# Another order of the seven block products of values and gates, and four pieces of work moved beside them

## The chip, the cores and the metric

The kernel runs on one core of a Trainium2 chip. The metric is the device time of one execution in microseconds (us), lower is better. The engines named here are TensorE (PE), the vector engine (DVE), the scalar engine (ACT), GpSimd (POOL), which here only issues DMAs, and SyncE (SP), whose queue loads the weights.

## The reference

One layer of a decoder with two branches that read the same normalised input: 512 tokens, model width 1024, all in fp32.

```python
proj = rms_norm(x, norm_mix) @ w_in
rq, rk, rv, rg, cq, ckv, krope, gr, gm = jnp.split(proj, offsets, axis=-1)
# retention: 4 heads, 256 wide in q and k, 512 in v, decay per head
ro = retention(rope(rq), rope(rk) * 256 ** -0.5, rv)
ro = rms_norm(ro, ret_norm)                 # per head
a_ret = (ro * silu(rg)) @ w_br
# latent attention: 8 heads, q from cq, k and v from ckv, rotary key krope shared
a_mla = causal_block_attention(q, k, v) @ w_bm
mixed = sigmoid(gr) * a_ret + sigmoid(gm) * a_mla
x = x + mixed @ w_o
x = x + square(relu(rms_norm(x) @ w_up)) @ w_down
x = x + sigmoid(rms_norm(x) @ w_ple_gate) * (p @ w_ple)
```

The change touches the retention part (`rv`, `rg`, the scores, the product with `w_br`) and, in two places, the preparation of the attention's keys.

## The kernel before, in words

**Matmuls in three parts.** An fp32 operand is split into a high part (ACT, L260 for weights, a rounding copy to the PE's fp32r type) and a low part (DVE, the difference: L264, or L266 where the weight is taken with the sign turned, which is the case for products 1 and 4). A product is then three matmuls, low by high, high by low, high by high, all on line L167 (`MM`). Names: `wr_` is the raw weight tile, `wh_` and `wl_` its high and low part; `xn0h`, `xn0l` are those of the normalised input.

**The order of the work.** A list of steps is written out by hand (`step(key, fn, ...)`), and `run_steps` goes through it. A step with a key uses one weight chunk of 512 KB; before the step runs, its chunk and the next one are split (`AHEAD` is 1), and, for the chunks of the products, the next three are loaded (`PREP` is 3). Matmuls stay in this written order; each other engine gets its instructions in an order that a scheduler makes from the same list, and works it off in order. There are 6 raw tiles (`NRAW`) and 3 of each part (`NW`).

**Values and gates by seven products.** For each pair of heads q = 0, 1 the values (`rv`) and then the gates (`rg`) are one matrix product of 2 x 2 blocks, computed with seven block products instead of eight (`ret_seven`). The operands made from the inputs are `xn` and sums of them (`s30`, `s50`, `s60`, `s70`...); those of the weights are made on the way to the chip. Each product p has two chunks c = 0, 1, with 12 matmuls each. The order before is 1, 7, 2, 6, 4, 5, 3. `wr_rv071` is chunk 1 of product 7 of the values of pair 0.

- Weights: SP loads 1, 2, 3 alone. 7 is loaded by SP, and POOL adds a second block to it (an accumulating DMA, L222). 6 has no tile of its own: POOL adds a block to 7's tile once 7 has been split, and 4's to the same tile once 6 has been split. 5 is loaded by SP and added to by POOL.
- PSUM: 1, 6, 5, 3 accumulate one after the other in the same two banks (chain a), 7 and 4 in two others (chain c), 2 in two of its own (b).
- Take-out (`seven_out`): after 1, 7 and 6 ACT copies the banks out (L749); after 2, 5 and 4 DVE adds them to what was taken out before (L754, tiles `cv` for values and `z` for gates, `_11`, `_21`, `_22` by block); after 3 ACT finishes the last block (L793, L785 with the silu for gates). The next product of a chain can start when the former has been taken out.

**Retention around it.** `qk(h, "rq", n)` and `"rk"` are projections of 24 matmuls with a rotary on DVE behind them (L809 to L816, then the split L306: `rqx`, `rqy`). `ret_scores` is 24 smaller matmuls (`rs`), loads the head's decay tile `dec` on SP's queue (L822), multiplies by it (L830) and splits the result (`ath`, `atl`). `ret_attend` multiplies scores and values (`ro`), `ret_gated` (L851, on DVE) multiplies the output `o` by its norm and by the gates `z`, `ret_turned` turns it with 16 transposes on PE (`ot`) and splits it with a gain (`rog`, ACT L308, DVE L311), and `branch_r` (`br`) multiplies it by `w_br`, in four steps of 24 matmuls each for a head. `gate_r` (`gr`) are eight projections for the branch's gate, `EARLY` of them in the first part of the kernel.

**The attention's part.** `scores` goes block by block over four blocks of queries (`sc`), six matmuls a block; `head_factor(h)` (`pbk`) spreads the norm factors of head h's keys with four transposes, from `hr`, which DVE works out (L602); `rotary_key` spreads a factor in the same way (`prho`) and makes the shared rotary key. `fill(n)` puts in n half projections of the gates (`gm`, later `gr`), 12 matmuls each.

Of the kernel before, what the change touches and what calls it, by code (L numbers as in the profile page):

```python
# [54 lines left out]
NDYN, NKEEP, NW, NRAW, NDRAW, AHEAD, PREP, EARLY, PAD = 45, 16, 3, 6, 4, 1, 3, 5, 104  # L55
# [91 lines left out]
def trunk_layer(ctx: ExitStack, tc: tile.TileContext, xT, pT, pos, gains, const, decay, wstream, outT):  # L147
# [58 lines left out]
    def step(key, fn, *args):  # L206
        steps.append((key, fn, args))
# [906 lines left out]
    def fill(n=1):  # L1114
        for _ in range(n):
            if fillers and fillers[0][0] is None:
                step(*fillers.pop(0))
            if fillers:
                step(*fillers.pop(0))
# [17 lines left out]
    step(("qr", 0), query_rotary, 0)  # L1137
    step(None, mask_parts)
    step(None, rotary_out, 0)
    fill(1)  # L1140
    step(None, rotary_key)
    fill(2)
    step(None, rotary_stats, 0)
    step(None, pair_sums, 0)
    fill(1)
# [6 lines left out]
    for h in range(MH):  # L1152
        p, more = h // 2, h + 2 < MH
        if h % 2 == 0 and h:
            step(None, scores, h, (0, 1))
            step(None, head_factor, h)
            step(None, scores, h, (2, 3))
            step(None, head_factor, h + 1)
        else:
            step(None, scores, h)  # L1160
        if h % 2 == 0:
            if more:
                step(("kq", h + 2), kq_head, h + 2)
            else:
                fill(2)
            if h:
                step(None, attend, h - 1)
            if more:
                step(("kq", h + 3), kq_head, h + 3)
            else:  # L1170
                fill(1)
            if h == 2:
                step(("qr", 1), query_rotary, 1)
            if h == 0:
                fill(1)
            step(None, transposes, h)
            if h:
                fill(1)
            if h == 2:
                step(None, rotary_out, 1)  # L1180
        else:
            if more:
                step(None, pair_sums, p + 1)
                step(("v", p + 1), value_pair, p + 1)
            else:
                fill(1)
            step(None, attend, h - 1)
            if more:
                if h == 3:
                    fill(1)  # L1190
                    step(None, rotary_stats, 1)
                step(None, pair_stats, p + 1)
            fill(1)
            step(None, transposes, h)
            fill(1)
        for i in range(3 if h >= 6 else 0):
            step(None, mo_split, 3 * (h - 6) + i)
# [15 lines left out]
    def qk(h, key, n):  # L1213
        step((key, h, n), ret_qk, h, key, n)

    def branch(h, *ks):
        for k in ks if h >= 0 else ():
            step(("br", h, k), branch_r, h, k)

    for q in range(RH // 2):  # L1220
        h = 2 * q
        qk(h, "rq", 0)
        if q:
            step(None, ret_turned, h - 1)
        qk(h, "rq", 1)
        branch(h - 1, 0)
        qk(h, "rk", 0)
        branch(h - 1, 1)
        qk(h, "rk", 1)
        for kind in ("rv", "rg"):  # L1230
            for p in (1, 7, 2, 6, 4, 5, 3):
                for c in range(2):
                    step(("sw", (kind, q), p, c), ret_seven, kind, q, p, c)
                if (kind, q) == ("rv", 0) and p in (1, 7, 2):
                    step(None, x_operand, {1: 6, 7: 5, 2: 3}[p])
                if (kind, p) == ("rv", 1):
                    branch(h - 1, 2)
                    step(None, ret_scores, h)
                    branch(h - 1, 3)
                if (kind, p) == ("rg", 1):  # L1240
                    step(None, ret_attend, h)
                if (kind, p) == ("rg", 4):
                    step(None, ret_gated, h)
        qk(h + 1, "rq", 0)
        step(None, ret_turned, h)
        qk(h + 1, "rq", 1)
        qk(h + 1, "rk", 0)
        branch(h, 0)
        qk(h + 1, "rk", 1)
        branch(h, 1)  # L1250
        step(None, ret_scores, h + 1)
        step(None, odd_v, h + 1)
        branch(h, 2, 3)
        step(None, ret_attend, h + 1)
        step(None, ret_gated, h + 1)
    for n in range(8):
        step(None, reload, n)
    for n in range(EARLY, 8):
        step(("gr", n), gate_r, n)
        if n == EARLY:  # L1260
            step(None, ret_turned, RH - 1)
    for k in range(4):
        step(("br", RH - 1, k), branch_r, RH - 1, k)
# [113 lines left out]
```

## Time and profile before

| what | us |
|---|---|
| median of 3 runs (lowest, highest) | 1119.35 (1118.16, 1121.62) |
| the profiled execution | 1118.9 |
| its span, first to last instruction | 1117.1 |
| PE busy | 1098.4 |
| DVE busy | 711.4 |
| ACT busy | 541.1 |
| POOL busy | 90.4 |

The granted clock of PE was 0.999 over the span. PE runs 5137 matmuls. A matmul of 512 columns has a row of 0.39 us in the timeline, though the next starts 0.23 us later, since they overlap; lengths of stages are therefore read from start to start. In the list of waits a row names the waiting engine and tile, then the instruction that ended the wait with its line, then the sum, the count and the longest in us.

### The profile page before, as it was taken

The page shows a single profiled execution, that of the slowest core. Times are in us where ns is not written, and L with a number is a line of the kernel's source. Part 1 is how long each engine was busy: PE and PEld are TensorE (multiplying, and loading weights), DVE is VectorE, ACT ScalarE, POOL GpSimd, SP SyncE. Part 2 cuts the span into 40 slices and gives each one's busy share as a digit, 9 for nine tenths or more (in the row PEclk, how much of TensorE's full clock was granted, in tenths as well). Part 3 has the DMA queues.
Part 4 walks back from the last instruction along what each step waited for, and adds up shares of the span by engine and source line. Part 5 has one row for each costly group of instructions (what it writes and reads, how often), then busy time and mean ns, then how long its engine had stood idle before and what let it go on. Part 6 is the DMA issues. An engine that isn't in the chain of part 4 may idle for free.

```text
span 1117.1 us, 13841 instructions
## 1 busy us (share of the span) xinstructions
PE 1098.4 (98%) x5137; PEld 909.6 (81%) x5137; DVE 711.4 (64%) x1135; ACT 541.1 (48%) x785; POOL 90.4 (8%) x121
## 2 busy tenths in 40 slices
PE   9999999999999999999999999999999999999998
PEld 7877878888878788887878877788888888888887
DVE  7697677566774655646456467555466666668785
ACT  7637556453465635345554644434444443444552
POOL 0000000001102001031100100010100100101000
PEclk9999999999999999999999999999999999999999
DMA  7242231466779734488873934693855765737511
GB/s 263 63 136 76 64 104 57 141 208 220 185 189 241 196 124 169 108 195 209 205 212 96 281 121 145 197 265 116 178 161 166 177 168 152 185 129 195 163 57 57
DMA packets 59860, 178.02 MB, mean 159 GB/s; under 512 B 7376, under 2 KB 8784, under 8 KB 59536
## 3 DMA queue, kind: packets, MB, share of 16 engines
q1 hardware_dynamic: 45168, 129.66, 35.1%
q0 software_dynamic: 14480, 47.46, 21.7%
q8 instruction: 40, 0.66, 0.2%
q14 instruction: 28, 0.23, 0.1%
q10 hardware_dynamic: 144, 0.03, 0.0%
HBM read 157.97 MB, written 17.04 MB: 157 GB/s over the span
## 4 chain that ended last, share of the span: by engine, by line
PE 75%; DMA 9%; DVE 6%; issue 5%; ACT 2%; POOL 1%; SPq 0%; POOLq 0%; ACTq 0%; DVEq 0%
PE up L167 16%; PE dn L167 14%; PE br L167 5%; DMA wr_rg<-wstream 5%; PE pg L167 4%; PE bm L167 4%; PE wo L167 4%; PE gr L167 3%; PE rq L167 3%; PE rk L167 3%; PE gm L167 3%; PE rg L167 2%; DMA wr_rv<-wstream 2%; PE sc L167 2%; PE rv L167 2%
## 5 line engine op out<-in xcount | busy, mean ns | idle before, releaser
L167 PE MATMUL dn<-wh_dn,cl 128*128 128x512 f32 x224 | 87.2, 389 | 0.0
L167 PE MATMUL dn<-wh_dn,ch 128*128 128x512 f32 x224 | 87.1, 389 | 0.0
L167 PE MATMUL dn<-wl_dn,ch 128*128 128x512 f32 x224 | 87.1, 389 | 0.0
L260 ACT ACTIVATE wh_dn<-wr_dn 128x1024 fp32r<-128x1024 f32 x32 | 34.0, 1062 | 74.5 <-PE up L167 54.3
L260 ACT ACTIVATE wh_up<-wr_up 128x1024 fp32r<-128x1024 f32 x32 | 34.0, 1061 | 58.8 <-PE up L167 29.3
L264 DVE TENSOR_TENSOR wl_dn<-wr_dn,wh_dn 128x1024 fp32r<-128x1024 f32 x32 | 39.1, 1221 | 25.8 <-ACT wh_dn L260 25.8
L264 DVE TENSOR_TENSOR wl_up<-wr_up,wh_up 128x1024 fp32r<-128x1024 f32 x32 | 39.1, 1223 | 18.8 <-ACT wh_up L260 18.8
L167 PEld LDWEIGHTS dn<-wl_dn,ch 128*128 128x128 f32 x224 | 42.0, 188 | 8.8
L167 PEld LDWEIGHTS dn<-wh_dn,cl 128*128 128x128 f32 x224 | 42.0, 188 | 8.7
L167 PEld LDWEIGHTS dn<-wh_dn,ch 128*128 128x128 f32 x224 | 42.0, 188 | 8.6
L982 DVE SCALAR_TENSOR_TENSOR f<-up,bcx 128x512 f32<-128x512 f32 x32 | 20.6, 686 | 44.4 <-PE up L167 44.4
L260 ACT ACTIVATE wh_dn<-dr_dn 128x1024 fp32r<-128x1024 f32 x24 | 25.4, 1060 | 44.3 <-PE up L167 29.4
L264 DVE TENSOR_TENSOR wl_dn<-dr_dn,wh_dn 128x1024 fp32r<-128x1024 f32 x24 | 29.4, 1223 | 24.5 <-ACT wh_dn L260 24.5
L222 POOL DMA_DIRECT2D dr_dn<-wstream x24 | 21.1, 892 | 294.0 <-DVE wl_dn L264 107.5
L260 ACT ACTIVATE wh_rg<-wr_rg 128x1024 fp32r<-128x1024 f32 x28 | 29.4, 1059 | 30.6 <-DMA wr_rg<-wstream 15.5
L260 ACT ACTIVATE wh_rv<-wr_rv 128x1024 fp32r<-128x1024 f32 x28 | 29.4, 1059 | 29.7 <-DMA wr_rv<-wstream 7.2
L264 DVE TENSOR_TENSOR wl_rg<-wr_rg,wh_rg 128x1024 fp32r<-128x1024 f32 x20 | 24.3, 1224 | 20.6 <-ACT wh_rg L260 20.4
L264 DVE TENSOR_TENSOR wl_rv<-wr_rv,wh_rv 128x1024 fp32r<-128x1024 f32 x20 | 24.3, 1223 | 14.0 <-ACT wh_rv L260 14.0
L1040 DVE TENSOR_TENSOR d<-d,dn 128x1024 f32<-128x1024 f32 x24 | 29.3, 1219 | 6.0 <-PE dn L167 6.0
L264 DVE TENSOR_TENSOR wl_br<-wr_br,wh_br 128x1024 fp32r<-128x1024 f32 x16 | 19.5, 1220 | 21.2 <-ACT wh_br L260 21.2
L260 ACT ACTIVATE wh_br<-wr_br 128x1024 fp32r<-128x1024 f32 x16 | 16.9, 1059 | 31.7 <-PE rk L167 16.3
L871 ACT ACTIVATE rt<-br 128x512 f32<-128x512 f32 x24 | 13.9, 594 | 25.5 <-PE br L167 25.5
(1819 smaller groups left out, 3449.2 us busy)
## 6 DMA issues: line engine op xcount, KB each, us to landing
wr_up<-wstream SPq DMA_DIRECT2D x32, 512.0 KB, 4.1
wr_dn<-wstream SPq DMA_DIRECT2D x32, 512.0 KB, 3.5
dr_dn<-wstream POOLq DMA_DIRECT2D x24, 512.0 KB, 7.0
wr_rv<-wstream SPq DMA_DIRECT2D x20, 512.0 KB, 4.2
wr_rg<-wstream SPq DMA_DIRECT2D x20, 512.0 KB, 4.8
wr_rv<-wstream POOLq DMA_DIRECT2D x16, 512.0 KB, 7.1
wr_rg<-wstream POOLq DMA_DIRECT2D x16, 512.0 KB, 7.9
wr_br<-wstream SPq DMA_DIRECT2D x16, 512.0 KB, 3.6
```

Of the source, the lines that this page charges most:

```text
L167: return tc.keep_in_program_order(nc.tensor.matmul(*a, **k))
L222: nc.gpsimd.dma_start(raw, chunk(("w", blk, kb, fb, c)), accum_op=ALU.add)
L260: i = ACT(hi, raw, AF.Copy, scale=sign)
L264: TT(lo, raw, hi.bitcast(F32), op=ALU.subtract)
L871: ACT(t, ps, AF.Copy)
L982: STT(u[:, i], ps[:, i], 0.0, V["bcx2"], op0=ALU.max, op1=ALU.mult)
L1040: TT(to, to, dps[p], op=ALU.add if sign > 0 else ALU.subtract)
```

## The change

1. The seven products run as 1, 7, 2, 6, 5, 4, 3. Between 6 and 5 stands one piece of other work: `ret_scores(0)` in the values of pair 0 (it stood behind 1), a branch step of head 1 in the values of pair 1 (it stood behind the retention scores there), and the first projection of the next head's queries in the gates of both pairs (it stood behind 3).
2. `ret_turned` stands behind both projections of the queries instead of behind the first; the branch steps and the key projections follow it in turn. For the last head it stands one `gate_r` later.
3. For the heads 2, 4 and 6 of the attention three blocks of scores stand before `head_factor` instead of two.
4. `rotary_key` stands behind the second of three fillers instead of the first.

```diff
--- before.py
+++ after.py
@@ -1137,9 +1137,9 @@
     step(("qr", 0), query_rotary, 0)
     step(None, mask_parts)
     step(None, rotary_out, 0)
+    fill(2)
+    step(None, rotary_key)
     fill(1)
-    step(None, rotary_key)
-    fill(2)
     step(None, rotary_stats, 0)
     step(None, pair_sums, 0)
     fill(1)
@@ -1152,9 +1152,9 @@
     for h in range(MH):
         p, more = h // 2, h + 2 < MH
         if h % 2 == 0 and h:
-            step(None, scores, h, (0, 1))
+            step(None, scores, h, (0, 1, 2))
             step(None, head_factor, h)
-            step(None, scores, h, (2, 3))
+            step(None, scores, h, (3,))
             step(None, head_factor, h + 1)
         else:
             step(None, scores, h)
@@ -1220,30 +1220,36 @@
     for q in range(RH // 2):
         h = 2 * q
         qk(h, "rq", 0)
+        qk(h, "rq", 1)
         if q:
             step(None, ret_turned, h - 1)
-        qk(h, "rq", 1)
+        qk(h, "rk", 0)
         branch(h - 1, 0)
-        qk(h, "rk", 0)
+        qk(h, "rk", 1)
         branch(h - 1, 1)
-        qk(h, "rk", 1)
         for kind in ("rv", "rg"):
-            for p in (1, 7, 2, 6, 4, 5, 3):
+
+            for p in (1, 7, 2, 6, 5, 4, 3):
                 for c in range(2):
                     step(("sw", (kind, q), p, c), ret_seven, kind, q, p, c)
                 if (kind, q) == ("rv", 0) and p in (1, 7, 2):
                     step(None, x_operand, {1: 6, 7: 5, 2: 3}[p])
                 if (kind, p) == ("rv", 1):
                     branch(h - 1, 2)
-                    step(None, ret_scores, h)
+                    if q:
+                        step(None, ret_scores, h)
+                elif (kind, p) == ("rv", 6):
                     branch(h - 1, 3)
-                if (kind, p) == ("rg", 1):
+                    if not q:
+                        step(None, ret_scores, h)
+                elif (kind, p) == ("rg", 1):
                     step(None, ret_attend, h)
-                if (kind, p) == ("rg", 4):
+                elif (kind, p) == ("rg", 6):
+                    qk(h + 1, "rq", 0)
+                elif (kind, p) == ("rg", 4):
                     step(None, ret_gated, h)
-        qk(h + 1, "rq", 0)
+        qk(h + 1, "rq", 1)
         step(None, ret_turned, h)
-        qk(h + 1, "rq", 1)
         qk(h + 1, "rk", 0)
         branch(h, 0)
         qk(h + 1, "rk", 1)
@@ -1257,7 +1263,7 @@
         step(None, reload, n)
     for n in range(EARLY, 8):
         step(("gr", n), gate_r, n)
-        if n == EARLY:
+        if n == EARLY + 1:
             step(None, ret_turned, RH - 1)
     for k in range(4):
         step(("br", RH - 1, k), branch_r, RH - 1, k)
```

Where the rows below carry numbers, a name's last number only tells tiles of one name apart.

DVE in the values of pair 0, from the weights of product 4 (before) and of product 5 (now). Before:

```order
L266 SCALAR_TENSOR_TENSOR wl_rv040_3365<-wr_rv070_3091,wh_rv040_3364 128x1024
L306 TENSOR_TENSOR rv0111l_3332<-cv01_11_3174,rv0111h_3331 128x512
L306 TENSOR_TENSOR s31l_3344<-sx1_2793,s31h_3343 128x512
L266 SCALAR_TENSOR_TENSOR wl_rv041_3388<-wr_rv071_3137,wh_rv041_3387 128x1024
L264 TENSOR_TENSOR wl_rv050_3407<-wr_rv050_3368,wh_rv050_3406 128x1024
L264 TENSOR_TENSOR wl_rv051_3435<-wr_rv051_3391,wh_rv051_3434 128x1024
L754 TENSOR_TENSOR cv00_21_3383<-cv00_21_3383,rv070_3240 128x512
L754 TENSOR_TENSOR cv01_21_3385<-cv01_21_3385,rv071_3241 128x512
L264 TENSOR_TENSOR wl_rv030_3453<-wr_rv030_3410,wh_rv030_3452 128x1024
```

Now:

```order
L264 TENSOR_TENSOR wl_rv050_3323<-wr_rv050_3266,wh_rv050_3322 128x1024
L264 TENSOR_TENSOR wl_rv051_3390<-wr_rv051_3307,wh_rv051_3389 128x1024
L830 TENSOR_TENSOR s00_3352<-rs00_3345,dec0_3343 128x512
L266 SCALAR_TENSOR_TENSOR wl_rv040_3407<-wr_rv070_3091,wh_rv040_3406 128x1024
L306 TENSOR_TENSOR atl_86<-s00_3352,ath_85 128x512
L830 TENSOR_TENSOR s01_3363<-rs01_3356,dec0_3343 128x384
L830 TENSOR_TENSOR s02_3374<-rs02_3367,dec0_3343 128x256
L830 TENSOR_TENSOR s03_3385<-rs03_3378,dec0_3343 128x256
L306 TENSOR_TENSOR atl_86<-s01_3363,ath_85 128x384
L306 TENSOR_TENSOR atl_86<-s02_3374,ath_85 128x256
L306 TENSOR_TENSOR atl_86<-s03_3385,ath_85 128x256
L266 SCALAR_TENSOR_TENSOR wl_rv041_3431<-wr_rv071_3137,wh_rv041_3430 128x1024
```

The two splits of 5 stand ahead of those of 4, and the multiplications of head 0's scores by the decay tile, with the splits of the scores, stand between them; the additions to `cv` for block 22 (product 5) and block 21 (product 4) have changed places and follow later.

POOL's DMAs in the gates of pair 0 (L222 are the accumulates, L353 stores values to memory for head 1). Before:

```order
L222 DMA wr_rg070_3498<-wstream 128x1024
L222 DMA wr_rg071_3525<-wstream 128x1024
L353 DMA v2d_3471<-cv00_22_3271 128x512
L353 DMA v3d_3474<-cv01_22_3273 128x512
L222 DMA wr_rg050_3732<-wstream 128x1024
L353 DMA v0d_3515<-cv00_12_3513 128x512
L353 DMA v1d_3519<-cv01_12_3517 128x512
L222 DMA wr_rg070_3498<-wstream 128x1024
L222 DMA wr_rg051_3755<-wstream 128x1024
L222 DMA wr_rg071_3525<-wstream 128x1024
L222 DMA wr_rg070_3498<-wstream 128x1024
L222 DMA wr_rg071_3525<-wstream 128x1024
```

Now:

```order
L222 DMA wr_rg070_3498<-wstream 128x1024
L353 DMA v2d_3425<-cv00_22_3225 128x512
L353 DMA v3d_3428<-cv01_22_3227 128x512
L222 DMA wr_rg071_3525<-wstream 128x1024
L353 DMA v0d_3515<-cv00_12_3513 128x512
L353 DMA v1d_3519<-cv01_12_3517 128x512
L222 DMA wr_rg070_3498<-wstream 128x1024
L222 DMA wr_rg050_3732<-wstream 128x1024
L222 DMA wr_rg071_3525<-wstream 128x1024
L222 DMA wr_rg051_3735<-wstream 128x1024
L222 DMA wr_rg070_3498<-wstream 128x1024
L222 DMA wr_rg071_3525<-wstream 128x1024
```

Both accumulates of 5 now stand beside those of 6 (third and fourth on the tiles of 070 and 071 come last in both); the stores v2d and v3d stand between the two accumulates of 7 and no longer behind them.

DVE where the outputs of head 0 are turned. Before:

```order
L264 TENSOR_TENSOR wl_rk_1_0_3946<-wr_rk_1_0_3943,wh_rk_1_0_3945 128x1024
L809 TENSOR_TENSOR rqa10_3903<-rq10_3878,trc_931 128x512
L810 TENSOR_TENSOR rqb10_3904<-rq10_3878,trs_932 128x512
L264 TENSOR_TENSOR wl_br_0_0_3991<-wr_br_0_0_3988,wh_br_0_0_3990 128x1024
L311 SCALAR_TENSOR_TENSOR rog00l_3913<-ot00_3907,gn_81,rog00h_3912 128x512
L311 SCALAR_TENSOR_TENSOR rog01l_3922<-ot01_3916,gn_81,rog01h_3921 128x512
L311 SCALAR_TENSOR_TENSOR rog02l_3931<-ot02_3925,gn_81,rog02h_3930 128x512
L311 SCALAR_TENSOR_TENSOR rog03l_3940<-ot03_3934,gn_81,rog03h_3939 128x512
L809 TENSOR_TENSOR rqa11_3974<-rq11_3949,trs_932 128x512
L810 TENSOR_TENSOR rqb11_3975<-rq11_3949,trc_931 128x512
L815 TENSOR_TENSOR rqa10_3903<-rqa10_3903,rqa11_3974 128x512
L816 TENSOR_TENSOR rqb10_3904<-rqb10_3904,rqb11_3975 128x512
```

Now:

```order
L264 TENSOR_TENSOR wl_br_0_0_3991<-wr_br_0_0_3988,wh_br_0_0_3990 128x1024
L809 TENSOR_TENSOR rqa11_3938<-rq11_3913,trs_932 128x512
L810 TENSOR_TENSOR rqb11_3939<-rq11_3913,trc_931 128x512
L815 TENSOR_TENSOR rqa10_3784<-rqa10_3784,rqa11_3938 128x512
L816 TENSOR_TENSOR rqb10_3785<-rqb10_3785,rqb11_3939 128x512
L311 SCALAR_TENSOR_TENSOR rog00l_3958<-ot00_3952,gn_81,rog00h_3957 128x512
L306 TENSOR_TENSOR rqx1l_3945<-rqa10_3784,rqx1h_3944 128x512
L311 SCALAR_TENSOR_TENSOR rog01l_3967<-ot01_3961,gn_81,rog01h_3966 128x512
L306 TENSOR_TENSOR rqy1l_3949<-rqb10_3785,rqy1h_3948 128x512
L264 TENSOR_TENSOR wl_rk_1_1_4026<-wr_rk_1_1_4023,wh_rk_1_1_4025 128x1024
L311 SCALAR_TENSOR_TENSOR rog02l_3976<-ot02_3970,gn_81,rog02h_3975 128x512
L311 SCALAR_TENSOR_TENSOR rog03l_3985<-ot03_3979,gn_81,rog03h_3984 128x512
```

The whole rotary of the queries of head 1 (rqa, rqb) now stands ahead of the low parts of the turned outputs, and its splits (rqx1l, rqy1l) and the second weight split of the keys among them.

## The prediction

> **What bounds the kernel now.** I read the page's first part, then TensorE's waits, then the stages in which the waits lie.
>
> ```profile
> PE 1098.4 (98%) x5137; PEld 909.6 (81%) x5137; DVE 711.4 (64%) x1135; ACT 541.1 (48%) x785; POOL 90.4 (8%) x121
> ```
>
> TensorE (PE) is busy 1098.4 us of a span of 1117.1. The change adds no matmul and removes none, so only what stands between the matmuls can move. What that is, the waits of PE say (us in total, times, longest):
>
> ```profile
> PE ot L167 <- DVE o L851: 2.2, 5, 0.9
> PE rg L167 <- DVE wl_rg L266: 1.7, 3, 0.8
> PE gm L167 <- DVE wl_gm L264: 1.6, 1, 1.6
> ...
> PE pbk L167 <- DVE hr L602: 1.0, 1, 1.0
> PE rv L167 <- DVE cv L754: 0.9, 2, 0.4
> PE rg L167 <- DVE z L754: 0.9, 2, 0.4
> ...
> PE rv L167 <- DVE wl_rv L266: 0.5, 1, 0.5
> ```
>
> These seven rows are 8.8 us, and each belongs to a place that the change touches: the transposes of the gated outputs (ot), the weights of products 1 and 4 (L266 splits only these), a filler (gm), the head factor (pbk), and the take-out of a product from PSUM before the next may use the chain (cv, z). A listed wait is shorter than what the stage loses, because the matmuls around it also lose their pipelining; so the terms below are lengths of stages against undisturbed ones.
>
> **The four blocks of products.** A chunk row of the chain of waits gives the undisturbed pace, 5.44 / 24 = 0.2267 us a matmul:
>
> ```profile
> 401.87 5.44 PE rk L167 x24
> ```
>
> Products 4, 5, 3 are three times 24 matmuls, 16.32 us. Windows from the first matmul of 4 to the first behind 3, in the order values and gates of the first pair of heads, values and gates of the second (length, PE busy, granted clock, DMA share, GB/s; the count takes in neighbours at the edges):
>
> ```profile
> 323.05:341.18 18.13, 17.19 (x74) 1.00 0.75 211
> 369.74:389.06 19.32, 17.47 (x73) 1.00 0.74 223
> 516.85:534.35 17.50, 16.94 (x73) 1.00 0.81 217
> 562.91:580.57 17.66, 16.91 (x74) 1.00 0.69 227
> ```
>
> The losses are 1.81, 3.00, 1.18 and 1.34, together **7.33 us**, at a granted clock of 1.00, so no throttle is in them. Two causes share them. First, 4's weights are late: they are 6's tile turned once more by an accumulating DMA of GpSimd (POOL), which may start only when 6's low part has been split off the tile, and then lands and is split itself. Secondly, 5 and 3 use the same PSUM chain back to back, so 3 stands until the vector engine (DVE) has taken 5 out.
>
> The new order 6, other work, 5, 4, 3 takes both away. Between 6's end and 4's start now lie 5 (5.44 us) and the other work (24 matmuls of a branch or projection, 5.44, or the retention scores of head 0, which took 4.06 in a window below), so 4's weights have over 9 us more; the longest loss so far was 3.00 in a whole block. 5 and 3 now have 4 between them, 5.44 us against two vector adds (the windows' loss holds one wait of 0.4 for them). 6 and 5 also share a chain, and here the other work stands between; I take 0 for that, since two copies of the scalar engine (ACT) on tiles half as wide as the 1.06 splits below are far under 4. 5 itself doesn't hang on a turned tile: its tile is loaded anew and its accumulate is issued before 4's. Bounds: 0 to 7.33 saved; I take 7.3, since the cover is longer than the loss in all four.
>
> **The turned outputs and the head factor.** Windows: the 16 transposes undisturbed, then for head 1, then for head 3; block 2 of the scores of head 4; the retention scores of head 0.
>
> ```profile
> 394.51:396.17 1.66, 1.66 (x17) 1.00 0.13 52
> 450.48:453.02 2.54, 2.10 (x18) 1.00 0.00 0
> 641.98:646.36 4.38, 2.50 (x17) 1.00 0.03 13
> 161.61:162.70 1.09, 1.09 (x10) 1.00 0.57 212
> 302.64:306.70 4.06, 4.06 (x26) 1.00 0.85 153
> ```
>
> Transposes: 2.54 − 1.66 = 0.88 and 4.38 − 1.66 = 2.72, **3.6 us**. They wait for the gated outputs (o, L851). Each now stands one projection of 5.44 us later, twice the larger loss; o has no new work ahead of it on DVE at heads 1 and 3. At heads 0 and 2 the distance from the gating to the turning shrinks by a product (4 is now next to last), from three times 5.44 to two, 10.9 us; there was no wait there, and the gating is four operations of 0.75. I take 0 there.
>
> Head factor of head 4: the wait is 1.0 in the list. Block 2 of the scores moves ahead of it, and its six matmuls last 1.09, so **1.1 us** of the loss is filled. At heads 2 and 6 there was no wait, and the score that moved ahead only makes the factor later by the same 1.09; I take 0, and 0.5 for each as the bound.
>
> **Rotary key.** The filler's wait of 1.6 is the low part of its weights, split on DVE. In the order of DVE nothing ahead of that split changes, and PE has the same matmuls before it but for the four of the rotary statistics, which go behind. So 0; bounds are a gain of 1.6, and a loss of 0.7 (one DVE operation of 128x512, as the row of 0.68 below) for what is queued behind.
>
> **What is exposed by the moves.** The retention scores of head 0 leave the place behind product 1, so everything up to 6 starts 4.06 us earlier (window above). 6's tiles are 7's, accumulated by POOL:
>
> ```profile
> 301.32 0.87 POOL L222 DMA_DIRECT2D wr_rv<-wstream  x1 [1.68 <-DVE wl_rv L264]
> 303.06 0.85 POOL L222 DMA_DIRECT2D wr_rv<-wstream  x1 [0.87 <-DVE wl_rv L264]
> 315.47 0.86 POOL L222 DMA_DIRECT2D wr_rv<-wstream  x1 [11.55 <-DVE wl_rv L264]
> 317.80 0.85 POOL L222 DMA_DIRECT2D wr_rv<-wstream  x1 [1.48 <-DVE wl_rv L264]
> ```
>
> ```profile
> 309.69 1.06 ACT L260 ACTIVATE wh_rv<-wr_rv 128x1024 fp32r<-128x1024 f32 x1 [1.20 <-issue]
> ...
> 312.86 1.05 ACT L260 ACTIVATE wh_rv<-wr_rv 128x1024 fp32r<-128x1024 f32 x1
> ...
> 321.07 1.06 ACT L260 ACTIVATE wh_rv<-wr_rv 128x1024 fp32r<-128x1024 f32 x1 [2.30 <-DMA wr_rv<-wstream]
> ...
> 324.59 1.06 ACT L260 ACTIVATE wh_rv<-wr_rv 128x1024 fp32r<-128x1024 f32 x1 [1.41 <-DMA wr_rv<-wstream]
> ```
>
> And PE's first matmul of 6:
>
> ```profile
> 317.61 0.39 PE L167 MATMUL rv<-wh_rv,s60l 128*128 128x512 f32 x1
> ```
>
> The first pair of POOL rows feeds 6 (high parts at 309.69 and 312.86), the second feeds 4 (321.07 and 324.59). 6 began at 317.61 and will begin at 313.55 on the old clock; its second chunk's low part is used from 313.55 + 13 x 0.2267 = 316.5. It is there at 312.86 + 1.06 + 1.22 = 315.1 (high and low split): a margin of 1.4 us. Bounds: no wait, if the accumulate takes what it took, 9.8 us from 303.06 on; and with the time of 4's second, 324.59 − 317.80 = 6.8, still none. But the decay tile and the next load of the SP queue move into this stretch, and the DMA engines were 0.85 busy there (window above). Against harm speaks how the transfers followed each other (SP's issues, then two rows of the page on its loads, with the median us to landing):
>
> ```profile
> 306.28 6.09 SPq L232 DMA_DIRECT2D wr_rv<-wstream  x2
> 323.42 6.89 SPq L232 DMA_DIRECT2D wr_rg<-wstream  x4
> ...
> wr_rv<-wstream SPq DMA_DIRECT2D x20, 512.0 KB, 4.2
> wr_rg<-wstream SPq DMA_DIRECT2D x20, 512.0 KB, 4.8
> ```
>
> A load was issued on SP at 306.28 while 6's two accumulates were under way, and their splits stand 3.2 us apart; 4's had no load beside them and stand 3.5 apart. I allow one new wait of the size of the listed one for 4, **0.5 us**.
>
> [...]
>
> **Sum.** 7.3 + 3.6 + 1.1 + 0 − 0.5 = 11.5. The profiled execution took 1118.9 (span 1117.1 and 1.8 around it), so 1107.4. The median of the runs, 1119.35, lies 0.45 above that execution: **1107.9 us**.
>
> **Rivals.**
>
> *6's accumulate is late* in the first block. If the second lands a whole load of this block later, 4.2, then 4.2 − 1.4 = 2.8 us are lost: 1110.7. For: the engines were near full there. Against: the spacing above. Chance 0.13.
>
> *DVE is squeezed between turning and branch.* Only one projection (5.44) now lies between the transposes and the branch that reads them, where there were two, and the low parts of the outputs share DVE with the rotary of the projection before:
>
> ```profile
> 395.32 0.68 DVE L810 TENSOR_TENSOR rqb<-rq,trs 128x512 f32<-128x512 f32 x1
> 395.92 1.22 DVE L264 TENSOR_TENSOR wl_br<-wr_br,wh_br 128x1024 fp32r<-128x1024 f32 x1
> 397.05 0.74 DVE L311 SCALAR_TENSOR_TENSOR rog00l<-ot,gn,rog00h 128x512 fp32r<-128x512 f32 x1
> ```
>
> By DVE's new order, six rotary operations of 0.61 from start to start, four outputs of 0.66 and one weight split of 1.13 end 7.4 us behind the projection, some 8 with the start and the handover. The branch starts 1.66 + 5.44 = 7.1 behind it and reads the third output six matmuls on, at 8.5, the fourth at 9.2. So it fits by about 1 us. If a second weight split (1.22) gets between, each of three places could lose about 1.2: 1107.9 + 3.6 = 1111.5. Chance 0.08.
>
> *4's wait is no matter of time given.* If the split of 4 stood in ACT's or DVE's order behind work that moves with it, the weight part would stay: listed 2.2 of 4.0, so 7.3 x 2.2 / 4.0 = 4.0, and 1111.9. Against: ACT waited 2.30 and 1.41 for the DMA itself. Chance 0.07.
>
> *The filler's wait goes too:* 1107.9 − 1.6 = 1106.3. Chance 0.02.
>
> *Two or three of the first three together:* up to 1107.9 + 2.8 + 3.6 + 4.0 = 1118.3, no change. Chance 0.05.
>
> *Slower: the raw buffers run short.* There are six. The two of the turned tile are now held through 5 as well, one product longer, while 5's own two wait beside them; 3's loads and the next block's find two left, and SP's queue is served in order, so a load that waits for a buffer holds all behind it. With two buffers a load of 4.8 and the two splits, 2.3, come to 7.1 a chunk pair against 5.44 of work: 1.7 for each pair late, over the two pairs of 3 and 1, so 3.4 in each of four blocks, 13.6 in all. That only undoes the gain, 1121.5. The kernel is slower from 14.9 on (1107.9 + 14.9 = 1122.8), 3.7 a block; that takes a third late pair, 7's, with which it is 5.1 a block: 1107.9 + 20.4 = 1128.3. Against: between 5 and 3 PE now spends 5.44 on 4, which needs no load. Chance 0.04.
>
> **How the numbers follow.** The forecast itself has 0.61; its own range is 1106.0 to 1110.5: 1.9 below, if the filler's 1.6 and part of the allowed 0.5 go as well, and 2.6 above, for a wait of 0.5 in five of the places above. The range 1105.5 to 1113.0 takes in the first four rivals and leaves out the last two, 0.09, and the forecast's tails. A measurement of this kernel tells 0.3%, 3.4 us, from no change. Faster: 0.61 + 0.13 + 0.08 + 0.07 + 0.02 = 0.91; same 0.05; slower 0.04.
>
> **What would show it.** Right: TensorE's waits no longer list ot on o, rv and rg on L266 for 4, nor cv or z on L754; the three last products and the other work run at 0.2267 a matmul; pbk waits 0.1 or less; gm still waits 1.6. The first rival shows as a wait of rv on wl_rv (L264) at the start or middle of 6 in the first block; the second as br on rog (L311); the third as rv or rg on L266; the slower one as ACT waiting for wr_rg of product 3 or 1, with SP's issue late. I am wrong if PE's busy time itself grows, or if the waits go and the span falls by less than 9.

## The result

The changed kernel takes **1105.86 us** (median of 4 runs, 1105.24 to 1106.31); the kernel before, on the same chip, 1119.57 (4 runs). The ratio is **0.9878**, with a 95% interval of 0.9865 to 0.9891: 13.7 us faster. The profiled execution took 1106.31, with a span of 1104.5, so between the two profiled executions 12.6 us lie, where the prediction had 11.5; the interval of the ratio, 12.2 to 15.1 us, holds both 12.6 and 13.7.

The list of PE's waits in the changed kernel, whole (us in total, times, longest):

```profile
PE gm L167 <- DVE wl_gm L264: 1.6, 1, 1.6
PE zero L167 <- DVE zero L360: 1.5, 1, 1.5
PE sc L167 <- ACT sqk L525: 0.8, 1, 0.8
PE gm L167 <- DVE mx L642: 0.6, 1, 0.6
PE pt0a L167 <- DVE p L651: 0.6, 1, 0.6
PE wo L167 <- DVE wl_o L264: 0.6, 1, 0.6
PE pA L167 <- DVE xg1l L311: 0.3, 1, 0.3
PE pA L167 <- ACT xg1h L308: 0.3, 1, 0.3
```

Of the seven rows that the prediction started from, six are gone: ot, both rows of L266, pbk, cv and z. The filler's 1.6 stays. And one row is gone that the prediction did not touch: `up` on `xr` (L932, 0.8 before).

Products 5, 4, 3 of the four blocks in the changed kernel (length, PE busy, granted clock, DMA share, GB/s), against 18.13, 19.32, 17.50 and 17.66 for 4, 5, 3 before:

```profile
322.55:338.89 16.34, 16.34 (x74) 1.00 0.79 229
372.89:389.21 16.32, 16.32 (x73) 1.00 0.56 194
510.67:526.99 16.32, 16.32 (x74) 1.00 0.86 196
560.99:577.31 16.32, 16.32 (x74) 1.00 0.55 190
```

The undisturbed length is 16.32, so the blocks' 7.3 us are saved to the last tenth. The transposes of the last head take 1.66 (from 638.72 to 640.38), as the undisturbed ones did before; those of heads 0, 1 and 2 too.

Two margins that the prediction had estimated can be read. (A margin is the time between the end of an operand's making and its first use.) First 6's high parts on ACT in the first block:

```profile
308.87 1.06 ACT L260 ACTIVATE wh_rv<-wr_rv 128x1024 fp32r<-128x1024 f32 x1 [0.26 <-DMA wr_rv<-wstream]
...
312.74 1.06 ACT L260 ACTIVATE wh_rv<-wr_rv 128x1024 fp32r<-128x1024 f32 x1 [1.76 <-PE rv L167]
```

The second ends its low part at 313.83 + 1.23 = 315.1, and PE, which begins 6 at 313.25, reads it at 313.25 + 13 x 0.2267 = 316.2: 1.1 us to spare, where 1.4 had been worked out. Then the low parts of the turned outputs of head 0, on DVE, and their reader on PE:

```profile
401.58 0.74 DVE L311 SCALAR_TENSOR_TENSOR rog03l<-ot,gn,rog03h 128x512 fp32r<-128x512 f32 x1
...
403.45 0.39 PE L167 MATMUL br<-rog02l,wh_br 128*128 128x512 f32 x1
```

The last low part ends at 402.32, 7.66 behind the projection that ended at 394.66 ("7.4 behind the projection, some 8 with the start"). PE reads the third part at 403.45, which DVE had finished by 401.66: 1.8 us to spare, where "about 1 us" had been worked out.

### The profile page after: what moved, and what is told of

It reads as the page before. It is cut to its first block, busy times and chain, and to the rows that moved or that the text cites. A ratio compares the mean times of both kernels' runs of the same rounds, so it can differ in the third digit from the quotient of the medians.

```text
span 1104.5 us, 13845 instructions
## 1 busy us (share of the span) xinstructions
PE 1093.7 (99%) x5137; PEld 910.8 (82%) x5137; DVE 711.1 (64%) x1135; ACT 541.1 (49%) x785; POOL 89.9 (8%) x121
## 4 chain that ended last, share of the span: by engine, by line
PE 92%; DVE 4%; ACT 1%; issue 1%; DMA 1%; SPq 0%; DVEq 0%; ACTq 0%
PE up L167 16%; PE dn L167 14%; PE rv L167 7%; PE rg L167 7%; PE br L167 6%; PE pg L167 4%; PE gr L167 4%; PE rk L167 4%; PE bm L167 4%; PE rq L167 4%; PE wo L167 4%; PE gm L167 3%; PE ro L167 2%; PE sc L167 2%; PE pcq L167 1%; PE rs L167 1%
## 5 line engine op out<-in xcount | busy, mean ns | idle before, releaser
L260 ACT ACTIVATE wh_rg<-wr_rg 128x1024 fp32r<-128x1024 f32 x28 | 29.6, 1059 | 31.1 <-PE rg L167 12.1
L222 POOL DMA_DIRECT2D dr_dn<-wstream x24 | 21.1, 890 | 289.4 <-DMA dr_dn<-wstream 165.0
```

What stands on the lines that cost most here:

```text
L222: nc.gpsimd.dma_start(raw, chunk(("w", blk, kb, fb, c)), accum_op=ALU.add)
L260: i = ACT(hi, raw, AF.Copy, scale=sign)
```

## The experiments

Each job ran its kernels beside the kernel before on one chip. The medians of before in these jobs were 1119.53, 1117.83, 1119.07 and 1119.80, so kernels of different jobs are compared by their ratios and by the stages of their traces, not by their microseconds.

### The products alone

```diff
-            for p in (1, 7, 2, 6, 4, 5, 3):
+            for p in (1, 7, 2, 6, 5, 4, 3):
 ...
# ret_scores(0), branch(h - 1, 3) and qk(h + 1, "rq", 0) between 6 and 5, as in the change;
# ret_turned, head_factor, rotary_key as before
```

> Only the new order of the seven products with the other work between 6 and 5; the turned outputs, the head factor and the rotary key stay as before. The theory of the prediction: the whole 7.3 us of the four blocks are saved here, no wait is left on the splits of product 4 (L266) nor on cv or z (L754), the transposes still lose 3.6 and the head factor 1.2. Added after the result: the first up product waited 0.94 us for the last output projection's take-out (xr, L932) before, and not after; in this kernel, as in the changed one, the last output projection lies in another PSUM bank than that product, so this wait should be gone too: 8.2 us in all, a ratio of 0.9926. Rival (4's wait is not a matter of time): about 3.3 saved, and rv or rg still wait on L266. Rival (6's accumulate late): a new wait of up to 2.8 on wl_rv of 6 in the first block.

Measured: 1108.77, ratio 0.9905 (0.9889 to 0.9921), 10.6 us. PE's waits in this kernel:

```profile
PE gm L167 <- DVE wl_gm L264: 1.5, 1, 1.5
PE zero L167 <- DVE zero L360: 1.5, 1, 1.5
PE pbk L167 <- DVE hr L602: 1.0, 1, 1.0
PE ot L167 <- DVE o L851: 1.0, 3, 0.3
```

No wait on L266, cv, z or xr, and none on wl_rv of 6: both rivals about the weights fall. More was saved than the expected 8.2 us (the ratio of 0.9926 lies outside the interval), and two reasons are in the traces. The transposes lost half of what they had lost before (1.0 listed instead of 2.2). Before, a gate's activation stood in ACT's queue in front of the copy of the retention output, and waited for its own reload from memory:

```profile
638.06 0.63 ACT L906 ACTIVATE ge<-ge 128x512 f32<-128x512 f32 x1 [2.42 <-DMA ge<-gr3d]
638.60 0.58 ACT L843 ACTIVATE o<-ro 128x512 f32<-128x512 f32 x1
```

The copy so began 1.9 us behind PE's last output matmul (636.31 + 0.39 = 636.70). In this kernel the same activation had waited 0.98, and the copy began 0.3 behind it (629.71 against 629.41). So part of the loss at the last head's turning was a late reload, not the length of the gating. The second reason is in the profiles of the experiments below that keep the old product order: most of them lost more in the products than the one profile of before.

### The turned outputs alone

```diff
-        if q:
-            step(None, ret_turned, h - 1)
         qk(h, "rq", 1)
+        if q:
+            step(None, ret_turned, h - 1)
 ...
-        if n == EARLY:
+        if n == EARLY + 1:
```

> Only the turned outputs one projection later (and for the last head one gate later), with the branch and key projections in the new turn. The theory of the prediction: 3.6 us saved, ratio 0.9968, ot no longer waits for o (L851), no wait of br on rog (L311); the first up product still waits for xr, since the banks of the last output projection and of it are the same as before. Rival (DVE squeezed between turning and branch): up to 1.2 us at each of three places given back, 0 to 1.2 saved, and br waits on rog.

Measured: ratio 0.9973 (0.9960 to 0.9986), 3.0 us, the interval from 1.6 to 4.5 holding the 3.6. No wait of ot is listed, and none of br on rog. What the products lost in this profile:

```profile
PE rg L167 <- DVE wl_rg L266: 2.7, 4, 0.8
...
PE rg L167 <- DVE wl_rg L264: 0.7, 1, 0.7
```

The first row was 1.7 before, and the second, a wait for 6's own weights, was not there. From start to start the products lose 9.7 us in this profile, against 7.35 in the profile of before. With the same product order, the weights of the gates were late by different amounts in these two profiles.

### The head factor alone

```diff
-            step(None, scores, h, (0, 1))
+            step(None, scores, h, (0, 1, 2))
             step(None, head_factor, h)
-            step(None, scores, h, (2, 3))
+            step(None, scores, h, (3,))
```

> Only the third block of scores ahead of the head factor for heads 2, 4, 6. The theory: 1.1 us saved (ratio 0.9990), pbk's wait of 1.0 falls to 0.1 or none, no new wait at heads 2 and 6. Rival: the later key factor makes the scores of the next head or the PSUM wait, up to 1.0 lost. The first up product still waits 0.8 for xr.

Measured: ratio 1.0000 (0.9988 to 1.0012), which holds the expected 0.9990. PE's list has no row of pbk any more, nor a new one in the attention; so the wait is gone, and its 1.1 us are inside what the timing can't tell from nothing. The profiled execution took 1122.13, and four of the twelve had a mean granted clock of 0.998 or less. This one shows where the clock fell: behind the waits in the last head's transposes, far from the head factor (windows as above: length, PE busy, granted clock, DMA share, GB/s).

```profile
643.15:646.55 3.40, 1.18 (x5) 1.00 0.02 8
646.56:649.97 3.41, 3.41 (x16) 0.50 0.41 144
```

### The rotary key alone

```diff
-    fill(1)
+    fill(2)
     step(None, rotary_key)
-    fill(2)
+    fill(1)
```

> Only the rotary key one filler later. The theory: nothing, since the filler's wait (gm on wl_gm, 1.6) is for a split that stands behind the same work on DVE as before; ratio 1.000, the wait stays at 1.6 (within 0.1), and the four matmuls of prho only stand behind the next filler. Rival: the wait goes too and 1.6 are saved (0.9986), or zm, now ahead of the key's own work, costs up to 0.7.

Measured: ratio 1.0001 (0.9989 to 1.0014); the wait of gm is listed with 1.6, as before and after. The prediction's 0 holds.

### Without the other work between 6 and 5

```diff
# the changed kernel, products 1, 7, 2, 6, 5, 4, 3
                     branch(h - 1, 2)
-                    if q:
-                        step(None, ret_scores, h)
-                elif (kind, p) == ("rv", 6):
+                    step(None, ret_scores, h)
                     branch(h - 1, 3)
-                    if not q:
-                        step(None, ret_scores, h)
 ...
-                elif (kind, p) == ("rg", 6):
-                    qk(h + 1, "rq", 0)
 ...
+        qk(h + 1, "rq", 0)
         qk(h + 1, "rq", 1)
```

> The changed kernel with the other work put back: products 1, 7, 2, 6, 5, 4, 3 without anything between 6 and 5 (retention scores and the branch steps behind product 1, the next head's query projection behind 3). The theory: 5 now follows 6 on the same PSUM chain at once, so it waits for ACT's two copies (0.6 each) as 3 waited for DVE's adds before, some 0.6 to 1.0 in each of four blocks, 2.4 to 4.0 in all; 4 keeps 5.44 us of cover, over its longest loss of 2.3, and does not wait. The last output projection falls in the first up product's bank again, so 0.94 for xr come back. Together 3.3 to 5 us more than the changed kernel. If the other work only moves and covers nothing, 0.9 more. If 4 needs both covers, 4.5 more on top.

Measured: 1108.45, ratio 0.9914 (0.9899 to 0.9929), against 0.9878 for the changed kernel. Windows of product 6, of 5, and of 4 and 3 together, in the first block:

```profile
316.26:321.87 5.61, 5.60 (x25) 1.00 0.97 185
321.87:327.50 5.63, 5.63 (x24) 1.00 0.81 263
327.50:338.38 10.88, 10.88 (x49) 1.00 0.93 245
```

6 and 5 lose 0.17 and 0.19, 4 and 3 nothing: 0.36 in this block and 1.4 in all four (their 6s last 5.61 each), where 2.4 to 4.0 were expected. The wait of `up` on `xr` is back with 0.8, as expected. So 5 alone covers 4's weights, and the other work is worth 1.4 us as a cover for the take-out of 6: ACT's copy of the first bank is done so nearly when PE wants it that PE's list has no row for it. The estimate by DVE's adds (0.69 each) was too high.

### 4 ahead of 5, with the other work

```diff
# the changed kernel
-            for p in (1, 7, 2, 6, 5, 4, 3):
+            for p in (1, 7, 2, 6, 4, 5, 3):
```

> The changed kernel with products 4 and 5 in the old order, the other work between 6 and 4: 1, 7, 2, 6, other, 4, 5, 3. The theory: 4's weights are covered by the other work alone (4.06 or 5.44 against losses of at most 2.3), and 3 behind 5 on the same chain waits for DVE's adds again, 0.43 listed and 0.69 lost in each of four blocks: 2.8 us more than the changed kernel. If 4's weights need the 5.44 of product 5 as well, more, with waits of rg on L266; if the order of 4 and 5 does nothing, no difference.

Measured: ratio 0.9916 (0.9901 to 0.9931). Its windows of 4, 5, 3 in the four blocks:

```profile
322.16:339.21 17.05, 16.62 (x75) 1.00 0.77 197
373.21:390.24 17.03, 16.60 (x73) 1.00 0.54 182
511.69:528.73 17.04, 16.61 (x73) 1.00 0.90 224
562.73:579.77 17.04, 16.61 (x74) 1.00 0.61 200
```

Each is 0.71 to 0.73 over 16.32, together 2.9 (expected 2.8). The list has cv and z with 0.9 each, and no row of L266. So the two causes are apart: the other work alone covers 4's weights, and the swap of 4 and 5 is what takes away 3's wait for 5. Either cover is enough for the weights.

### Five raw tiles

```diff
# the changed kernel
-NDYN, NKEEP, NW, NRAW, ... = 45, 16, 3, 6, ...
+NDYN, NKEEP, NW, NRAW, ... = 45, 16, 3, 5, ...
```

> The changed kernel with five raw weight tiles instead of six. The rival on the slower side held that the turned pair, kept through 5, leaves the loads too few tiles. The theory: in the changed kernel no load is the last thing a product waits for, and loads of 3 and of the next block end several us before their split; with one tile fewer some are late, 0 to 4 us in all, mostly in the gates. The rival: the tiles were at their limit already, so a sixth of them less costs over 5 us, seen as ACT waiting for wr_rg and PE for wl_rg of products 7, 2 or 5.

Measured: 1106.45, ratio 0.9896 (0.9879 to 0.9912). ACT waits more for the gates' loads than in the changed kernel, where this row has 4.7:

```profile
ACT wh_rg L260 <- DMA wr_rg<-wstream: 10.0, 5, 2.8
```

But PE's list has no row of rv or rg; the one new row of PE that lies in the weights is in the tail (dn, 0.8). So the raw tiles were not at their limit, and the rival on the slower side is refuted at its mechanism: even with a tile fewer, no product waits: from start to start all four blocks together lose less than 0.1 us.

### The branch right behind the turning

```diff
# the changed kernel, at both places
         step(None, ret_turned, h)
-        qk(h + 1, "rk", 0)
         branch(h, 0)
-        qk(h + 1, "rk", 1)
+        qk(h + 1, "rk", 0)
         branch(h, 1)
+        qk(h + 1, "rk", 1)
```

> The changed kernel with the branch step right behind the turned outputs, the key projection behind it: the cover between turning and branch is 0 instead of 5.44. It measures what the turned outputs need. From DVE's order and the times of one operation, the four low parts end 7.7 us behind the projection that stands ahead of the transposes (394.66 to 402.32 in the changed kernel), and the branch would read them from 1.9 to 4.0 behind it: the branch is late by 3.5 to 4.5 us at each of heads 0, 1 and 2, 10 to 14 us in all, with br waiting on rog (L311). That would also give the changed kernel's margin, 5.44 less that. If the squeeze rival had the queue right but too long, the loss is over 5.44 a place, 16 and more.

Measured: 1133.02, ratio 1.0136 (1.0121 to 1.0151), some 27 us over the changed kernel. The waits of the first place, and the largest:

```profile
PE rs L167 <- DVE rkx1l L306: 4.4, 1, 4.4
...
PE br L167 <- DVE rog02l L311: 1.4, 1, 1.4
...
PE br L167 <- DVE rog00l L311: 1.0, 1, 1.0
...
PE br L167 <- DVE rog01l L311: 0.3, 1, 0.3
```

Start to start the branch loses 1.29 + 0.47 + 1.60 = 3.4 at each of heads 0, 1 and 2, 10.1 in all, at the lower edge of the expected 10 to 14. The projection that stands there in the changed kernel lasts 5.44, so its margin is about 2.0, which agrees with the 1.8 read above. The rest was not foreseen: the retention scores now follow the last key projection at once and wait 4.4 us for its rotary, twice. And at three of these places matmuls ran at half the granted clock (the section on the hardware has rows of one). These stretches last 13.7 us in all, and PE is busy in 12.1 of them, which costs half of that, 6.0. So 10.1, 8.8 and 6.0 make up 24.9 of the 27 us.

### The bank of the last output projection

```diff
# the kernel before; e9_bank_off with 1 spare tile, e9_bank_on with 3
+    def spare(n):
+        ps = B(f"spare{n}")
+        MM(ps[:, 0:P], identr, identr, start=True, stop=True)
+        ACT(sm("spo"), ps[:, 0:4], AF.Copy)
+    for n in range(1):
+        step(None, spare, n)
     for k in range(4):
         step(("br", RH - 1, k), branch_r, RH - 1, k)
```

> The kernel before, with one spare PSUM tile put in ahead of the last head's branch (one small matmul and a copy of four columns, about 0.3 us in all), which turns the ring of banks by one: the last output projection moves from bank 0 to bank 4, while the first up product keeps banks 0 and 1. The theory that the 0.94 us of the first up product are a matter of the bank alone: PE's wait of up for xr (L932) is gone, 0.9 saved less 0.3. If they came from the order of work elsewhere, the wait stays at 0.8.

> The same with three spare tiles (about 0.9 us): the last output projection lies in bank 1, the second bank of the first up product's tile. The theory of the bank: the wait of up for xr stays at 0.8 as in the kernel before, so only the spare work is added. If spare work of itself takes the wait away, it is gone here too.

Measured: ratios 0.9993 (0.9980 to 1.0006) and 1.0002 (0.9988 to 1.0017), neither to be told from no change, as so small a term must be. In the list of waits they differ: with one spare tile the row of `up` is gone, with three it stands as before:

```profile
PE up L167 <- DVE xr L932: 0.8, 1, 0.8
```

In the programs of all twelve experiments and of the two kernels the last output projection lies in bank 0 or 1, the pair of the first `up` tile, or elsewhere: in the six where it lies there (before, the turned outputs, the head factor, the rotary key, no other work, three spare tiles) the row is listed, and in the eight others it is not. So the 0.94 us, which is what the listed 0.8 costs from start to start, come from the eight banks, which the new order of PSUM tiles hands out in another turn, and from nothing that the change was about: they were won by luck.

### The fillers ahead of the rotary

```diff
# the changed kernel
-    step(None, rotary_out, 0)
     fill(2)
+    step(None, rotary_out, 0)
     step(None, rotary_key)
     fill(1)
```

> The changed kernel with the two fillers ahead of the rotary of the queries instead of behind it (fill 2, rotary_out, rotary_key, fill 1). The theory of the prediction says that the filler's wait of 1.6 on its low part is DVE's order: eleven rotary operations of about 0.65 stand ahead of that split. With the filler's step first the split is issued before them, the wait of 1.6 should go and about 1.7 be saved; the rotary is then up to 1.2 later, and is first read by the scores 30 us on. If the wait only moves to the next split, behind the rotary now, nothing is saved.

Measured: 1112.08, ratio 0.9939 (0.9923 to 0.9955): slower than the changed kernel. The row of gm is gone, and two new ones stand in its place:

```profile
PE sqr L167 <- DVE sa L560: 2.8, 1, 2.8
PE st L167 <- ACT sums L587: 1.9, 1, 1.9
```

DVE did the four multiplications of the rotary only from 68.31 on, behind the filler's product (L686), and the statistics waited for them. The filler's wait was the cover of the rotary. The two waits are 3.1 us more than the 1.6 that went; by the ratios some 6.8 were lost. The profile has most of the rest: at the end of the first wait and behind it, from 72.53 to 79.36, the granted clock is 0.50. PE is busy in 6.5 us of that stretch, which costs 3.2.

### The rotary cut in two

```diff
# the changed kernel
-    step(None, rotary_out, 0)
+    step(None, rotary_mul, 0)      # the squares and the four multiplications
     fill(2)
+    step(None, rotary_out, 0)      # the sums and the splits
     step(None, rotary_key)
```

> The changed kernel with the rotary of the first queries cut in two steps: the two squares and the four multiplications stay where they were, the two sums, the square's sum and the splits go behind the two fillers. What the last run taught: the filler's wait covers DVE's rotary, and putting the whole rotary behind the fillers makes the statistics (sqr) wait for it instead. Here DVE does the filler's split after four of the eight operations that stood ahead of it: it should end at 66.9 on the clock of the changed kernel, where PE wants it at 67.7, so the wait of 1.6 goes; the square's sum ends at some 69.5, and the statistics want it at 70.6. So 1.7 us less than the changed kernel, 1104.2. If the other operations that move (zm of the filler, the splits of the rotary) push the square's sum past 70.6, part of it comes back as a wait of sqr.

Measured: 1106.39, ratio 0.9878 (0.9858 to 0.9897), no better than the changed kernel. On DVE all went as expected: the filler's split at 66.24, the square's sum ended at 69.4, no wait of gm and none of sqr. But PE's list begins with a wait two steps on:

```profile
PE st L167 <- ACT sums L591: 1.9, 1, 1.9
```

On ACT, in this kernel:

```profile
75.46 0.74 ACT L260 ACTIVATE wh_kq<-wr_kq 128x640 fp32r<-128x640 f32 x1 [4.09 <-PE gm L167]
76.11 0.61 ACT L305 ACTIVATE kph<-krot 128x512 fp32r<-128x512 f32 x1
76.62 0.58 ACT L591 ACTIVATE sums<-sums 128x512 f32<-128x512 f32 x1
```

The copy of the sums stands behind a weight split that waited 4.09 us until PE had finished with a filler's weights. So the 1.7 us went from DVE's queue to ACT's. The profiled execution was the longest of the five, 1108.24, and has a stretch at half pace behind that wait (below); by its wait alone the kernel is no faster than the changed one either. A version that beats the changed kernel was not found.

## Why the prediction was right, and where it was off

**The products, 7.3.** Right in mechanism and, for the profiled pair, in size: 16.32 to 16.34 in each block. The two causes it named are shown apart: without the swap 2.9 come back and only as waits for cv and z; without the other work only 1.4, and no wait for 4's weights. As a figure for the old order in general, 7.3 was low. In the profiles of the five experiments that kept it, the products lose 9.7, 8.9, 9.1, 8.7 and 7.0 us from start to start. The take-out has 2.7 to 2.8 of that each time; the late weights have 4.2 to 6.9, with waits for 6's as well in three of the five. So the one profile that the sum was made from, with 7.35, is one draw from a loss that varies, and the second lowest of six. In the new order the loss is 0.1 or less in all profiles that have both the swap and the other work, and ACT's waits for the gates' transfers (`wh_rg` on DMA `wr_rg`), 14.6 to 21.2 us in those six, are 4.7 in the changed kernel.

**The turned outputs, 3.6.** Right: 1.66 at each head after, and 3.0 us (1.6 to 4.5) alone. But as a figure this was one draw as well. Head 1 lost 0.87 or 0.88 in each of the six profiles that turn as before; the last head's loss follows the wait of ACT for the reload in front of the copy (`ge` on `gr3d`), which the prediction had not read. The table has both in us, the loss from the end of the projection ahead.

| profile | wait for the reload | loss of the last head's transposes |
|---|---|---|
| one spare tile, three spare tiles | none | 0.9, 0.9 |
| the products alone | 0.98 | 1.1 |
| the rotary key alone | 2.11 | 2.3 |
| before | 2.42 | 2.7 |
| the head factor alone | 2.99 | 4.3, half-pace stretch included |

The move covers the late reload all the same.

**Head factor, 1.1, and rotary key, 0.** Both right in the list of waits (from start to start the head factor's stage is 1.0 shorter); in time neither can be told from nothing, as the sizes say.

**The allowance for one new wait, 0.5.** Wrong: there is none. The margin for 6's second chunk was 1.1.

**What the sum lacked.** The 0.94 us of `up` on `xr`, far behind the change. The step that failed is the first one, which took the rows of the places that the change touches, and left the tail out. Against it stands the start of the kernel, where the first matmuls (`pA`) lost 0.75 more in this profiled execution; they wait there for the splits of the first inputs (`xg`), in every profile by a different amount. Profile against profile: 7.3 + 3.6 + 1.0 + 0.9 − 0.75 = 12.1, of 12.6.

**The medians.** Between them lie 13.7 us, 1.1 more than between the profiles. No run shows one cause for that: the products lose more in most profiles of the old order than in the one used here, the transposes less in most, and there is a third part that the prediction didn't have. In the four jobs of the experiments 14 of the 68 executions of the kernel before had a mean granted clock of 0.998 or less, and in each job the median of these is 1.3 to 3.5 us above that of the others. Of the 28 executions of five kernels with the new turning (the changed kernel, the turned outputs alone, no other work, 4 ahead of 5, five raw tiles) none had; the other three with the new turning make long waits of their own. In the one profile of such an execution with the old turning, of the head factor alone, the half-pace stretch lies behind the last head's transposes, whose waits the change takes away; where it lay in the others isn't shown. That the forecast came within 2.0 us of the median is in part luck: several terms were off, some one way and some the other.

**The rivals.** 6's accumulate late: refuted by the margin of 1.1, though narrow, and by the eight profiles with 5 ahead of 4 or with other work behind 6, none of which has a wait for 6's weights. DVE squeezed: refuted, margin 1.8 read and 2.0 by experiment. 4's wait not a matter of time: refuted by every run with a cover. The filler's wait going too: refuted twice. The raw buffers: refuted with a tile fewer.

**Loads beside accumulates.** In the traces the transfers took longer side by side: before, 6's second accumulate landed 9.3 us after its issue, with 6's first still under way for 6.1 of them and a load beside it that took 6.7; 4's two accumulates, with no load beside them, took 5.5 and 6.7, and the load at 312.04, nearly alone, 3.3. How much of the 9.3 is the load's isn't shown. The prediction had looked at the spacing of the splits, 3.2 against 3.5, which doesn't measure this, and the 9.8 us from which it worked out its margin had one load in them already. In the changed kernel both loads of 3 were issued while 6's second accumulate was under way (at 305.41 and 307.64; before, at 306.28 and 312.04, the second near its end): the loads took 7.4 and 6.2, and the accumulate 9.8. That is 0.5 more than before, where the first rival had 4.2, and no wait of PE came of it.

## What to carry to other kernels

Where a product waits both for its weights and for the take-out of the one before, find out which of two covers serves which wait: here either piece of work was enough for the weights; only the swap helped the take-out of 5, and only the other work that of 6. A wait that one engine's queue makes can be the cover of the next: taking the filler's 1.6 away gave 2.8 and 1.9 to the statistics in one order and 1.9 in another. And a term taken from one profile is one draw where the wait hangs on when a DMA lands: the products lost 7.0 to 9.7 us and the transposes 1.8 to 5.1 in six profiles of the same order. Several profiles of before would have shown this spread before the change was made.

## What the runs showed of the hardware

**A stall can be followed by a stretch at half pace.** In the profiled execution of the kernel with the rotary cut in two, windows of PE around the wait of 1.9 us (granted clock behind the count):

```profile
71.35:74.76 3.41, 3.41 (x19) 1.00 0.43 109
74.76:78.17 3.41, 1.53 (x9) 1.00 0.39 99
78.18:81.58 3.40, 3.40 (x9) 0.50 0.53 144
81.59:85.00 3.41, 3.41 (x17) 1.00 0.80 253
```

The wait ends at about 77.25, but the half-pace stretch begins only at 78.17 and lasts 3.41 us. PE is busy throughout it, with 9 matmuls (neighbours at the edges counted), where 3.41 us hold 15 at 0.2267 each; at half the clock half of it, 1.7 us, is lost on top of the wait. Behind the first wait of 4.4 us of the kernel with the branch right behind the turning:

```profile
422.85:426.25 3.40, 0.68 (x3) 1.00 0.24 54
426.26:429.66 3.40, 3.40 (x12) 0.50 0.67 259
429.67:433.08 3.41, 3.41 (x22) 1.00 0.00 0
```

In this kernel half-pace stretches begin at 426.26, 467.22 and 627.64, which lie 12 and 47 times 3.413 us apart, so in this profile they fall on a grid of that step. In the six cases on record (three here, one each with the rotary cut, the fillers first and the head factor alone) PE was busy for 0.6 to 1.7 us of the 3.41 just ahead. Behind the filler's wait of 1.55 in the kernel before the granted clock stayed at 1.00, with 1.9 us busy in the stretch that holds the wait (it begins 307 steps of 3.413 us ahead of 1114.95, where half pace begins at the end of that kernel's profile):

```profile
67.07:70.48 3.41, 1.86 (x9) 1.00 0.29 73
70.48:73.89 3.41, 3.41 (x24) 1.00 0.40 100
```

With the fillers first, one stretch with 1.5 us busy (79.36 to 82.77), right behind one at half pace, was not followed by half pace either; so the traces give no exact boundary. Only one execution of each kernel was traced, so why one execution has such a stretch and the next has none isn't shown. With the rotary cut in two, two of the five executions had a mean granted clock of 0.998 and took 1107.43 and 1108.24, the other three 0.999 and 1106.20 to 1106.39.

**The order of PSUM tiles decided a wait at the end of this program**: 0.94 us at `up`, by nothing but the bank that the last output projection came to lie in. Listed with 0.8 before, the wait was gone with one spare tile and listed with 0.8 again with three.
